# Block forms of the output projection made on GpSimd in an earlier stage, and the norm's sums on ScalarE

## The chip, the cores and the metric

The kernel runs on one core of one Trainium2 chip, as one launch. The time is device microseconds of that core, and the median over several runs. The five engines are named as the profile names them: PE is TensorE (matmuls), DVE is VectorE, ACT is ScalarE, POOL is GpSimd, SP is SyncE, which here only issues DMAs. PEclk is the clock that PE was granted, as a share of full speed.

## The reference

A decoder trunk of two layers over 1024 tokens of 1024 channels. Each layer projects x, runs a main mixer on 1024 channels (layer 0: causal pooling, layer 1: forgetting attention with 16 heads) and a cross-attention of 4 heads of 128 into 256 memory tokens, gates both, and multiplies the 1536 joined channels by `w_out`; then comes a layer norm. What the change touches is the end of layer 1 and its memory attention:

```python
    y_main = main_fn(u_main)
    y_mem = memory_attention(q_mem, mem, w_mem_kv)
    y = jnp.concatenate([y_main * jax.nn.silu(g_main), y_mem * jax.nn.silu(g_mem)], axis=-1)
    return y @ w_out
...
        x = layer_norm(ALPHA * x + y, ln_g[layer], ln_b[layer])

def layer_norm(x, g, b):
    mu = jnp.mean(xf, axis=-1, keepdims=True)
    var = jnp.mean(jnp.square(xf - mu), axis=-1, keepdims=True)
    y = (xf - mu) * lax.rsqrt(var + LN_EPS) * g.astype(jnp.float32) + b.astype(jnp.float32)
```

All arithmetic is float32 outside; inside, a float32 operand is split into a high and a low part of fewer bits, and a product takes three matmuls (high by high, high by low, low by high).

## The kernel before, in words

Layer 1 runs in this order: the memory part (`mem_attention`: keys, values and queries of the memory heads, then a loop over eight row tiles t with `probs(t)`, and two steps behind it `values`), the shared keys and values, the forgetting attention over 16 heads in 8 pairs (`fox`), and the output projection (`Seven.rest`). PE follows an order that is written out by hand (`manual_schedule`), and matmuls of a later stage are filled in between (`Fill`). For the other engines a scheduler sets the order, except for the instructions handed to `keep_in_program_order` (`pin`). Each engine works through its own queue in order, DMA issues included; a wait at the front of a queue holds all that is behind.

In the memory part the softmax runs for each t as: DVE's row maxima (L536, L537), ACT's exponentials (L540), DVE's sums and reciprocals (L543, L544), ACT's and DVE's high and low halves of the probabilities (L546, L547, tile P). Meanwhile weights for the next stage are loaded on SP and split by ACT and DVE (L171 and L172, L198 to L200, tiles w and MK). The outputs of the memory heads (tile V) are gated and stored in DRAM as `y1d[2]` by four DMAs on POOL's queue (L585), then read back at the end.

The output projection multiplies y (1024 by 1536) by W_out (1536 by 1024), both cut in half twice. The 512 memory channels (c = 2) are multiplied in the plain way, in four pairs of row tiles sp = 0 to 3: `heads_of(sp)` issues 48 matmuls for each (L806). The 1024 main channels (c = 0, 1) go in seven products instead of eight: W_out's 8 tiles of 128 rows are 4 sets (k) of 2 x 2 blocks, and of each set seven forms are wanted: the blocks 11, 21, 22 and 12 as "t3" = b22 - b12, and sums of these, "t2", "t4", "t1". Each form of each k is a pair of float16 halves (128 x 2 x 512, 256 KB), scaled by `swo`, a power of two that is known when layer 0's output projection has passed over W_out (L347); 28 pairs in all. In `four` and `block` raw blocks are loaded on SP into rows of the large tile `lines` (A in the profile, L739), summed on POOL, some on DVE (L769), turned into the high half on ACT (L777) and the low half on DVE (L778), into tiles of B, w, MK, R and V as these come free.

For each pair sp, `rows(sp)` makes the halves of y in the same seven forms: sums of absolute values on ACT (L863), added up on DVE (L864), the largest over the partitions through two small PE instructions (L334, DVE L335, PE L337, DVE L338), a scale from it, four sums on POOL (L874), then ACT (L171) and DVE (L172) halves. `seven(sp)` issues seven products of 48 matmuls (L895) and collects them on DVE (L905, L915, L922, L923). `opened` adds the residual to the heads' part (L944). Then `normed` takes mean and variance of each of the two row tiles with two statistics instructions (L1026) and small ones (L1028 to L1036) on DVE, and applies them on ACT and POOL (L1043 to L1045), the last tile on DVE (L1049, L1051). `between(sp, k)` sets which step of `rows` and `normed` lies between which products.

## Time and profile before

| what | us |
|---|---|
| median of 3 runs | 1208.27 |
| lowest and highest of them | 1206.38, 1209.21 |
| the profiled execution's own time | 1205.48 |
| its span, first to last instruction | 1203.8 |
| PE busy in the span | 1163.3 |
| DVE busy | 847.0 |
| ACT busy | 720.2 |
| POOL busy | 360.1 |

The stages that matter here: the memory part of layer 1 from 468 to 592 us, the heads stage of the output projection from 1050 to 1107 us, the seven products from 1107 to 1191 us, and the last norm to 1204 us. In a row of groups stand the line, the engine, the operation, the tile written and those read, the shape, the count, and then busy time, mean ns of one, and idle time of the engine just before them with what ended it. In a timeline row the first number is the start and the second the length, of all the instructions joined in the row where it ends in x2 or more. In a row of waits stand who waited, for whom, the total, the number of times and the longest.

### The profile page before, as it was taken

To read this page: it belongs to the slowest core of one execution; us is meant where nothing else is said; L and a number is where in the kernel's file an instruction comes from. 1 tells how busy PE (TensorE), PEld (TensorE's weight loads), DVE (VectorE), ACT (ScalarE), POOL (GpSimd) and SP (SyncE) were. 2 spreads that over 40 slices of the span, in tenths; PEclk is the share of its full clock that TensorE was granted. 3 is DMA by queue.
4 is the path that set the end of the run, shared out by engine and by line. 5 is a ranking of instruction groups with operands and counts; after the bars stand their busy time and mean duration, and the time that the engine had idled before them with its cause. 6 is when DMAs were issued, how large, how long until landed. Compare 5 with 4: busy or idle time off the path is not lost. (4 is left out here: it accounts for less than half of the span.)

```text
span 1203.8 us, 20044 instructions
## 1 busy us (share of the span) xinstructions
PE 1163.3 (97%) x6908; PEld 658.8 (55%) x6908; DVE 847.0 (70%) x1954; ACT 720.2 (60%) x1597; POOL 360.1 (30%) x476
## 2 busy tenths in 40 slices
PE   8999999999999999999999999999999999998985
PEld 5566766555555556556664555555555545454432
DVE  6744675555755557457655888778778788889898
ACT  6578875875674234566423767667667677765421
POOL 4322001310000000000012554555445445684554
PEclk8999999999999999999999999999999999998998
DMA  7576756854388555355725989979987999884011
GB/s 259 172 244 189 171 102 206 264 164 148 104 307 254 141 157 134 102 147 117 228 89 120 197 188 194 196 162 222 204 176 156 165 234 214 213 271 159 18 53 71
DMA packets 288663, 208.10 MB, mean 173 GB/s; under 512 B 225201, under 2 KB 238641, under 8 KB 288561
## 3 DMA queue, kind: packets, MB, share of 16 engines
q1 hardware_dynamic: 281584, 183.69, 61.2%
q0 software_dynamic: 6976, 23.14, 6.0%
q8 instruction: 54, 0.88, 0.3%
q14 instruction: 49, 0.39, 0.1%
HBM read 120.07 MB, written 22.61 MB: 119 GB/s over the span
## 5 line engine op out<-in xcount | busy, mean ns | idle before, releaser
L388 PE MATMUL pj<-A,w 128*128 128x512 f16 (+2 forms) x2848 | 653.2, 383 | 1.1 <-ACT w L198 1.1
L388 PEld LDWEIGHTS <-w 128*128 128x128 f16 (+1 forms) x2560 | 245.7, 98 | 277.8 <-issue 9.1
L1415 ACT ACTIVATE T<-MK,s 128x512 f32<-128x512 f32 x192 | 111.2, 579 | 65.4 <-DVE s L1407 48.4
L1444 DVE SCALAR_TENSOR_TENSOR P<-T,s,P 128x512 f16<-128x512 f32 x192 | 112.0, 613 | 39.9 <-ACT P L1443 38.1
L1443 ACT ACTIVATE P<-T,s 128x512 f16<-128x512 f32 x192 | 103.0, 576 | 53.4 <-issue 28.9
L1381 POOL TENSOR_SCALAR_AFFINE_SELECT raw<-R 128x256 f32<-128x256 f32 (+3 forms) x128 | 59.8, 469 | 181.1 <-DVE s L1407 100.1
L585 POOL DMA_DIRECT2D y1d<-V x4 | 2.1, 534 | 341.0 <-DMA B<-in_wk_dram 335.1
L199 DVE TENSOR_TENSOR w<-raw,w 128x512 bf16<-128x512 f32 x74 | 52.3, 707 | 60.7 <-ACT w L198 39.6
L352 PE MATMUL L<-A 128*128 128x512 f16 (+3 forms) x384 | 84.7, 326 | 5.9 <-DVE s L1407 5.8
L388 PEld LDWEIGHTS pj<-A,w 128*128 128x128 f32 x352 | 65.1, 188 | 17.3 <-ACT w L198 1.9
L352 PEld LDWEIGHTS <-A 128*128 128x128 f16 x384 | 37.4, 98 | 49.3 <-issue 8.1
L178 POOL TENSOR_TENSOR w<-B,w 128x512 f16<-128x512 f32 x54 | 62.9, 1166 | 4.0
L644 PEld LDWEIGHTS <-T 128*128 128x128 bf16 x384 | 36.9, 98 | 45.8 <-issue 1.9
L198 ACT CAST w<-raw 128x512 fp32r<-128x512 f32 x76 | 46.7, 615 | 24.9 <-DMA raw<-in_win_dram 10.7
L895 PEld LDWEIGHTS <-A 128*128 128x128 f16 x336 | 33.1, 99 | 44.8 <-issue 7.5
L1469 PEld LDWEIGHTS <-V 128*64 128x64 f16 (+1 forms) x1152 | 50.6, 104 | 12.9 <-issue 6.0
L1469 PE MATMUL O<-T,V 128*64 128x128 f16 (+1 forms) x1152 | 57.5, 220 | 0.0
L1407 DVE CUSTOM_DVE_ANT_0 MK<-L,R,scales 128x512 f32<-128x512 f32 x64 | 45.3, 708 | 9.7 <-PE L L352 9.4
L200 ACT CAST w<-raw 128x512 bf16<-128x512 f32 x78 | 48.2, 617 | 3.3 <-PE pj L388 1.9
L258 POOL DMA_DIRECT2D W<-in_win_dram x48 | 26.5, 553 | 55.9 <-ACT W L267 44.2
L540 ACT ACTIVATE P<-L,s 128x256 f32<-128x256 f32 x64 | 29.5, 472 | 22.9 <-DVE s L537 19.4
L267 ACT ACTIVATE W<-W 128x512 f32<-128x512 f32 (+1 forms) x68 | 42.2, 623 | 0.0
(388 smaller groups left out, 2092.6 us busy)
## 6 DMA issues: line engine op xcount, KB each, us to landing
raw<-in_win_dram SPq DMA_DIRECT2D x66, 256.0 KB, 3.5
W<-in_win_dram POOLq DMA_DIRECT2D x48, 256.0 KB, 4.1
A<-in_wout_dram SPq DMA_DIRECT2D x36, 256.0 KB, 4.2
R<-cumd SPq DMA_DIRECT2D x16, 512.0 KB, 4.7
B<-in_win_dram SPq DMA_DIRECT2D x15, 512.0 KB, 5.1
y0d<-Y SPq DMA_DIRECT2D x12, 512.0 KB, 4.1
raw<-in_wout_dram SPq DMA_DIRECT2D x24, 256.0 KB, 2.8
T<-y0d SPq DMA_DIRECT2D x12, 512.0 KB, 4.9
```

The lines of the kernel that those rows point to most:

```text
L178: pin(nc.gpsimd.tensor_tensor(to.lo, src, to.hi, ALU.subtract))
L198: pin(nc.scalar.copy(to.hi, src))
L199: pin(nc.vector.tensor_tensor(to.lo, src, to.hi.bitcast(F32), ALU.subtract))
L200: pin((top or nc.scalar.copy)(to.top, src))
L352: nc.tensor.matmul(acc, a, b, start=i == 0, stop=i == len(terms) - 1)
L388: nc.tensor.matmul(accs[n], a[:, k, :], b[:, pc * 4 + k, n * NH : (n + 1) * NH], start=seen[n] == 1, stop=seen[n] == 3 * KT,)
L1381: tc.keep_in_program_order(nc.gpsimd.affine_select(C[:, :w], R[:, lo:up], [[-1, w]], ALU.is_ge, -NEG, base=w - P, channel_multiplier=1,))
L1407: nc.vector.tensor_tensor_reduce(p[:, lo:up], lg, rows, unq, top, ALU.add, ALU.min, m[:, n : n + 1])
L1415: nc.scalar.activation(e, p[:, lo:up], AF.Exp, bias=top, scale=-1.0, accum_out=sums[:, n, hd % 2, i : i + 1],)
L1443: nc.scalar.activation(pair[:, lo:up], e, AF.Copy, scale=r)
L1444: nc.vector.scalar_tensor_tensor(pair[:, L + lo : L + up], e, r, pair[:, lo:up], ALU.mult, ALU.subtract)
L1469: nc.tensor.matmul(acc[rows, (i % 4) * P : (i % 4) * P + P], v[:, b, 2 * j : 2 * j + (1 if e else 2), :].rearrange("p e d -> p (e d)"), pt ...
```

## The change

The forms of W_out are made earlier. A generator, `blocks_of_w_out`, is handed to layer 1's `mem_attention` as `aside` and stepped at fixed places: before and after the memory keys, behind two of the heads, and at each step t. It works on POOL's queue alone, pinned: for each k it loads four raw blocks (256 KB each), scales them, makes the sums, makes high and low halves with a copy and a subtraction, and stores the seven pairs in a DRAM tensor `w7d`. That is 16 loads, 16 scalings, 16 sums, 28 copies, 28 subtractions and 28 stores.

At the end, `blocks(upto)` loads the 28 pairs on SP, ready for use, into rows of `lines`, and tiles w, V and R. The lines L739 to L778 of raw loads, sums and halves are gone.

Besides, the inputs of the third and fourth heads part are loaded and split before they are asked for, the rows x of the residual too, the gate product of the last head pair's first columns goes straight to where `rows(0)` reads it, and the order of the seven products becomes 11, 12, s2, s1, s3, s4, 22. The small constants of the shared keys' stage move to a row of `lines` and are made ahead of the generator. The loads of R in the attention are pinned from the third head on.

Last, for the first three pairs `normed_pair` replaces `normed`: the sum and the sum of squares of each row tile come from ACT passes with an accumulator, the small instructions work on both tiles at once (two columns), and the result is applied on ACT and POOL for the first tile and on DVE, with two passes of 1024 columns, for the second. The last pair keeps `normed`.

The diff, cut to its core:

```diff
+            every = lines[0][:, 15, :].bitcast(F32)
+            tc.keep_in_program_order(nc.gpsimd.memset(every[:, P : 2 * P], 1.0))
+            tc.keep_in_program_order(nc.gpsimd.affine_select(
+                every[:, :P], every[:, P : 2 * P], [[1, P]], ALU.is_ge, 0.0, base=0, channel_multiplier=-1,
+            ))
+            next(aside)
             for h in range(MH):
                 keys(h)
+            next(aside)
...
             vals(h)
+            if l:
+                next(aside)
...
             for t in range(ST + 2):
                 part = fill.left / (ST + 2 - t)
+                if aside:
+                    next(aside, None)
                 if t < ST:
                     probs(t)
                 if before and t == ST - 2:
...
             fill.pump(float("inf"))
+        if aside:
+            run(aside)
         if last:
             last(1)
...
+    BLOCKS = ("11", "21", "t2", "t1", "t3", "22", "t4")
+
+    def blocks_of_w_out():
+
+        gp, pin = nc.gpsimd.tensor_tensor, tc.keep_in_program_order
+
+        def ask(k):
+            at = [lines[0][:, 4 * (k % 2) + j, :].bitcast(F32) for j in range(4)]
+            for j, r in enumerate(at):
+                pin(nc.gpsimd.dma_start(r, wout[1, j % 2, 4 * (j // 2) + k]))
+            return at
+
+        def scale(rs):
+            for r in rs:
+                pin(nc.gpsimd.tensor_scalar(r, r, swo, 1.0, ALU.mult, ALU.mult))
+
+        asked, turn, done = ask(0), 0, []
+
+        def split(b, k, r):
+            nonlocal turn
+            row = lines[0][:, 8 + turn % 7, :].rearrange("p (e n) -> p e n", e=2)
+            turn += 1
+            pin(gp_copy(row[:, 0], r))
+            pin(gp(row[:, 1], r, row[:, 0], ALU.subtract))
+            done.append((w7d[BLOCKS.index(b), k], row))
+
+        def store():
+            while done:
+                pin(nc.gpsimd.dma_start(*done.pop(0)))
+
+        scale(asked)
+        pin(gp(asked[1], asked[3], asked[1], ALU.subtract))
+        yield
+        for k in range(4):
+            b11, b12, b21, b22 = asked
+            if k < 3:
+                asked = ask(k + 1)
+            if k:
+                scale((b11, b12, b21, b22))
+                pin(gp(b12, b22, b12, ALU.subtract))
+                yield
+                store()
+            split("11", k, b11)
+            pin(gp(b11, b12, b11, ALU.add))
+            split("t3", k, b12)
+            split("21", k, b21)
+            pin(gp(b21, b21, b11, ALU.subtract))
+            yield
+            store()
+            split("22", k, b22)
+            pin(gp(b22, b22, b11, ALU.subtract))
+            split("t2", k, b11)
+            split("t4", k, b21)
+            split("t1", k, b22)
+            yield
+            store()
+
...
-        def block(self, b, f, by=None):
-
-            pin = tc.keep_in_program_order
-            if not self.spare:
-                self.spare.extend(self.pieces())
-            to, r = self.spare.pop(0), f[b]
-            pin(nc.scalar.activation(to.hi, r, AF.Copy, scale=swo))
-            pin(nc.vector.scalar_tensor_tensor(to.lo, r, swo, to.hi, ALU.mult, ALU.subtract))
-            self.w7[b].append(to)
-            if b == "11":
-                self.gp(f["t2"], f["t3"], f["11"], ALU.add, by)
-            elif b == "21":
-                self.gp(f["t4"], f["21"], f["t2"], by=by)
-            elif b == "22":
-                self.gp(f["t1"], f["22"], f["t2"], by=by)
-
...
+        def blocks(self, upto):
+
+            while self.got < upto:
+                for pair in self.pieces():
+                    b, k = BLOCKS[self.got // 4], self.got % 4
+                    tc.keep_in_program_order(nc.sync.dma_start(pair, w7d[BLOCKS.index(b), k]))
+                    self.w7[b].append(Half(pair[:, 0], pair[:, 1]))
+                    self.got += 1
...
+            of = self.load(2, 2, self.more("R", F32))
+            yield
...
+            self.third = Split(MK([P, 4, 2 * P]), MK([P, 2, 4, 2 * P], BF16))
+            self.fourth = self.load(2, 3, sb([P, 4, 2 * P], "P", 4))
+            self.blocks(14)
+            yield
+            hi_lo(self.third, of, True)
+            self.z = [rows_of(x1, sp, self.make[sp]) for sp in range(2)]
...
-            add(z12, self.product(y["s4"], w["22"]), z12)
-            between(2)
             add(u, self.product(y["s2"], w["t2"]), u)
             nc.vector.tensor_tensor(z12, z12, u, ALU.add)
-            between(3)
+            between(2)
             p = self.product(y["s1"], w["t1"])
             add(z12, p, z12)
             add(z22, p, z22)
-            between(4)
+            between(3)
             add(v, self.product(y["s3"], w["t3"]), u)
             nc.vector.tensor_tensor(z22, z22, v, ALU.add)
             nc.vector.tensor_tensor(z21, z21, v, ALU.add)
+            between(4)
+            add(z12, self.product(y["s4"], w["22"]), z12)
...
+                if sp < n - 1:
+                    return normed_pair(sp, zs[sp], gb, dst, self.room[:, 14, :].bitcast(BF16))
                 for a in range(2):
-                    normed(2 * sp + a, zs[sp][a], gb, None, dst, 2 * sp + a < ST - 1)
...
-                self.split(22)
-                w = self.split_last()
+                accs, units = heads_of(2, self.third, (("L", 3), ("pj", 2), ("pj", 2), ("L", 3)))
+                self.blocks(28)
                 next(rows[0])
-                next(w)
                 run(islice(units, 28))
                 next(rows[0])
-                next(w)
                 run(islice(units, 10))
                 next(rows[0])
-                next(w)
                 run(units)
+                self.z.append(rows_of(resid, 3, self.make[3]))
                 zs[2] = opened(2, accs)
                 accs, units = heads_of(3, None, (("T", 2), ("T", 2), ("L", 3), ("O", 1)))
...
+    def normed_pair(sp, z, gb, dst, unread):
+
+            add, ss, v, sd, r, t = (tiny(2) for _ in range(6))
+            for a in range(2):
+                nc.scalar.activation(unread, z[a], AF.Copy, accum_out=add[:, a : a + 1])
+            nc.vector.tensor_scalar(add, add, -1.0 / D, None, ALU.mult)
+            for a in range(2):
+                nc.scalar.activation(unread, z[a], AF.Square, bias=add[:, a : a + 1], accum_out=ss[:, a : a + 1])
+            nc.vector.tensor_scalar(v, ss, 1.0 / D, LN_EPS, ALU.mult, ALU.add)
+            nc.scalar.activation(sd, v, AF.Sqrt)
+            nc.vector.reciprocal(r, sd)
+            nc.vector.tensor_tensor(t, r, r, ALU.mult)
+            nc.vector.tensor_tensor(t, t, v, ALU.mult)
+            nc.vector.tensor_scalar(t, t, -0.5, 1.5, ALU.mult, ALU.add)
+            nc.vector.tensor_tensor(r, r, t, ALU.mult)
+            nc.vector.tensor_tensor(t, add, r, ALU.mult)
+            nc.scalar.activation(z[0], z[0], AF.Identity, bias=t[:, 0:1], scale=r[:, 0:1])
+            nc.gpsimd.tensor_tensor(z[0], z[0], gb[0], ALU.mult)
+            nc.gpsimd.tensor_tensor(z[0], z[0], gb[1], ALU.add)
+            nc.vector.scalar_tensor_tensor(z[1], z[1], add[:, 1:2], gb[0], ALU.add, ALU.mult)
+            nc.vector.scalar_tensor_tensor(z[1], z[1], r[:, 1:2], gb[1], ALU.mult, ALU.add)
+            for a in range(2):
+                nc.sync.dma_start(dst[(2 * sp + a) * P : (2 * sp + a + 1) * P, :], z[a])
 
...
+                to = out_proj.first[1][:, 3, :] if (pr, k) == (7, 0) else o[:, cols]
+                tc.keep_in_program_order(nc.gpsimd.tensor_tensor(to, o[:, cols], g[:, cols], ALU.mult))
...
+            pin = tc.keep_in_program_order if hd > 2 else lambda ins: ins
+            pin(nc.sync.dma_start(R, cumd[hd].partition_broadcast(P)))
...
-        later_tags = iter([("B", 10)] * 3 + [("w", 6)] * 6 + [("MK", 4)] * 2 + [("R", 2)] * 2 + [("V", 4)] * 2 + [("B", 10)] * 2)
+        later_tags = iter([("", k) for k in range(8)] + [("w", 6)] * 6 + [("", k) for k in range(8, 16)] + [("V", 4)] * 2 + [("R", 2)])
```

POOL's queue in the memory part, before: the last loads of weights ahead of it (W), the four stores of the memory heads' output, and the first work of the next stage.

```order
L258 DMA W_2765<-in_wv_dram 128x512 x2
L258 DMA W_2786<-in_wv_dram 128x512 x2
L585 DMA y1d<-V_5065 128x1024
L585 DMA y1d<-V_5066 128x1024
L585 DMA y1d<-V_5067 128x1024
L585 DMA y1d<-V_5068 128x1024
L1264 MEMSET G_6222 128x128
L1265 AFFINE_SELECT G_6222<-G_6222 128x128
L176 TENSOR_SCALAR B_6336<-B_6336,scales 128x512
```

The same place after, where A is the tile `lines`: the start of the generator behind those loads,

```order
L741 DMA A_3344<-in_wout_dram 128x512 x4
L746 TENSOR_SCALAR A_3344<-A_3344,scales 128x512 x4
L763 TENSOR_TENSOR A_3344<-A_3344 128x512
L741 DMA A_3344<-in_wout_dram 128x512 x4
L193 TENSOR_SCALAR A_3344<-A_3344 128x512
L755 TENSOR_TENSOR A_3344<-A_3344 128x512
L775 TENSOR_TENSOR A_3344<-A_3344 128x512
L193 TENSOR_SCALAR A_3344<-A_3344 128x512
L755 TENSOR_TENSOR A_3344<-A_3344 128x512
```

and its end, with the stores of V:

```order
L193 TENSOR_SCALAR A_3344<-A_3344 128x512
L755 TENSOR_TENSOR A_3344<-A_3344 128x512
L193 TENSOR_SCALAR A_3344<-A_3344 128x512
L755 TENSOR_TENSOR A_3344<-A_3344 128x512
L760 DMA w7d<-A_3344 128x1024 x4
L598 DMA y1d<-V_5114 128x1024
L598 DMA y1d<-V_5115 128x1024
```

Between the two pieces stand 74 more rows of the same kinds: the stores of V, which stood right behind the weights' loads, are now behind all the generator's work.

DVE's queue in the heads stage, before, from the halves of the blocks (into MK) to the reduction L335 for the first pair's scale (L944 are the adds of `opened`, L199 a split of y's memory channels):

```order
L778 SCALAR_TENSOR_TENSOR MK_12767<-A_3343,scales,MK_12767 128x512 x2
L778 SCALAR_TENSOR_TENSOR MK_12776<-A_3343,scales,MK_12776 128x512 x2
L769 TENSOR_TENSOR A_3343<-A_3343 128x512
L864 TENSOR_REDUCE yscales<-yscales 128x1
L944 SCALAR_TENSOR_TENSOR A_3343<-A_3343,T_12695 128x512
L944 SCALAR_TENSOR_TENSOR A_3343<-A_3343,T_12696 128x512
L944 SCALAR_TENSOR_TENSOR A_3343<-A_3343,L_12697 128x512
L199 TENSOR_TENSOR T_12876<-T_12873,T_12875 128x1024
L944 SCALAR_TENSOR_TENSOR A_3343<-A_3343,O_12698 128x512
L944 SCALAR_TENSOR_TENSOR G_12865<-G_12865,L_12760 128x512
L944 SCALAR_TENSOR_TENSOR G_12865<-G_12865,pj_12761 128x512
L335 TENSOR_REDUCE yscales<-L_12813 1x1
```

After, the same two reductions of the scale (L864 is now L901) and the adds (now L981):

```order
L199 TENSOR_TENSOR T_12971<-P_12728,T_12970 128x1024
L981 SCALAR_TENSOR_TENSOR B_12758<-B_12758,O_12826 128x512
L901 TENSOR_REDUCE yscales<-yscales 128x1
L981 SCALAR_TENSOR_TENSOR G_12811<-G_12811,L_12879 128x512
L981 SCALAR_TENSOR_TENSOR G_12811<-G_12811,pj_12880 128x512
L335 TENSOR_REDUCE yscales<-L_12924 1x1
L981 SCALAR_TENSOR_TENSOR G_12812<-G_12812,pj_12881 128x512
L338 COPY yscales<-L_12924 128x1
L271 TENSOR_SCALAR yscales<-yscales 128x1
L272 TENSOR_SCALAR yscales<-yscales 128x1
```

The halves and sums of blocks are gone from between, and the reductions stand among adds alone.

ACT's queue among the seven products, before, where the first pair's norm takes a root for each tile (L1030), and applies it (L1043); L171 are halves of y, L907 a product's copy out of its bank:

```order
L1030 ACT_TABLE_LOAD
L1030 ACTIVATE s_13151<-s_13150 128x1
L907 ACTIVATE P_13186<-pj_13187,yscales 128x512
L1030 ACTIVATE s_13171<-s_13170 128x1
L171 ACTIVATE A_12641<-T_13018,yscales 128x512
L171 ACTIVATE A_12641<-T_13020,yscales 128x512
L1043 ACTIVATE G_12686<-G_12686,s_13153,s_13152 128x1024
L171 ACTIVATE A_12641<-raw_13141,yscales 128x512
L863 ACTIVATE A_12641,yscales<-T_13202 128x1024
L863 ACTIVATE A_12641,yscales<-T_13204 128x768
L1043 ACTIVATE G_12687<-G_12687,s_13173,s_13172 128x1024
```

After, with the four sums of `normed_pair` (L1061, L1064) and one root for both tiles (L1066):

```order
L171 ACTIVATE A_12713<-T_12809,yscales 128x512
L1061 ACTIVATE A_12713,s_13219<-G_12753 128x1024
L1061 ACTIVATE A_12713,s_13219<-G_12754 128x1024
L1064 ACTIVATE A_12713,s_13220<-G_12753,s_13219 128x1024
L944 ACTIVATE P_13245<-pj_13246,yscales 128x512
L1064 ACTIVATE A_12713,s_13220<-G_12754,s_13219 128x1024
L171 ACTIVATE A_12713<-T_13071,yscales 128x512
L1066 ACT_TABLE_LOAD
L1066 ACTIVATE s_13222<-s_13221 128x2
L171 ACTIVATE A_12713<-T_13073,yscales 128x512
L171 ACTIVATE A_12713<-raw_13212,yscales 128x512
```

Four passes of 1024 columns stand on ACT between halves of y where two roots stood.

More of the change, by code (lines that the diff above doesn't have):

```diff
@@ L795, in heads @@
+        got = 0
         def heads(self, accs, ys, apart=False):
@@ L963, in rest @@
                 next(rows[0])
+                next(rows[1])
+                self.z.append(rows_of(resid, 2, G))
+                self.blocks(22)
                 accs, units = heads_of(1, self.second, (("T", 2), ("T", 2), ("L", 3), ("O", 1)))
```

118 lines of the change are left out of this document (44 added, 74 removed).

## Prediction

> **What bounds the kernel now.** I read the page first, for the engine that is busy all the time, and then the stages that the change touches: how full each engine is in them, what TensorE (PE) waits for, and the prices of the groups.
>
> ```profile
> span 1203.8 us, 20044 instructions
> PE 1163.3 (97%) x6908; PEld 658.8 (55%) x6908; DVE 847.0 (70%) x1954; ACT 720.2 (60%) x1597; POOL 360.1 (30%) x476
> PEclk8999999999999999999999999999999999998998
> ```
>
> PE is busy for 97% of the span, and its order of instructions is the same before and after. So time is won only where PE stands idle or runs at a lower granted clock, which the last row shows in the two slices around 1085 us, and each new wait of PE is lost whole. The stages, as busy time in each stretch (for each engine us and count, then granted clock, DMA share, GB/s):
>
> ```profile
> core 0: us, PE busy (x) PEld busy (x) DVE busy (x) ACT busy (x) POOL busy (x), PEclk, DMA share, GB/s
> 468.00:530.00 62.00, 61.24 (x366) 36.91 (x364) 32.92 (x66) 34.85 (x62) 0.00 (x0) 1.00 0.51 136
> 530.00:592.00 62.00, 62.00 (x420) 36.77 (x418) 42.49 (x111) 41.16 (x117) 0.00 (x0) 1.00 0.66 148
> 592.00:604.00 12.00, 11.76 (x133) 9.46 (x129) 10.12 (x15) 2.79 (x7) 2.96 (x7) 1.00 1.00 343
> 1050.00:1107.00 57.00, 51.62 (x275) 28.75 (x274) 53.08 (x75) 35.47 (x62) 39.17 (x28) 0.94 0.75 235
> 1107.00:1191.00 84.00, 76.11 (x342) 33.65 (x340) 77.93 (x151) 29.73 (x51) 43.14 (x21) 0.98 0.12 44
> ```
>
> 468 to 592 is layer 2's memory part, with PE full, POOL empty and DVE at 32.92 and 42.49 of 62. 1050 to 1107 is the heads stage and 1107 to 1191 the seven products: there DVE is nearly full (53.08 of 57, 77.93 of 84), and PE loses 5.4 and 7.9 us. PE's waits from 1050 us to the end (total, times, longest):
>
> ```profile
> PE L L337 <- DVE yscales L335: 7.1, 3, 2.5
> PE pj L895 <- DVE G L905: 2.5, 2, 2.3
> PE pj L895 <- DVE A L905: 1.3, 1, 1.3
> PE L L334 <- DVE yscales L864: 1.2, 1, 1.2
> PE O L806 <- DVE G L1488: 0.8, 1, 0.8
> ```
>
> Every wait is for DVE. And in the timeline of PE in the heads stage:
>
> ```profile
> 1077.47 0.61 PE L806 MATMUL L<-B,T 128*128 128x512 bf16 x2
> 1087.48 0.58 PE L337 MATMUL L<-yscales,ones 1*128 1x1 f32 x2 [2.22 <-DVE yscales L335]
> 1087.99 1.22 PE L806 MATMUL L<-B,T 128*128 128x512 f32 x2
> ```
>
> After the 2.22 us of idleness a pair of matmuls takes 1.22 us instead of 0.61: the granted clock falls for some 6 us after a long wait. In the first row of the two, 0.94 of 57 us, that is 3.4 us.
>
> **The change, part by part.**
>
> *Heads stage.* What DVE spends here on the blocks' lo halves (L778, first row) and DVE's and POOL's share of the blocks' sums (L769, second row):
>
> ```profile
> 1050.00:1107.00 57.00, 27.24 (x27) 0.94 0.75 235
> 1050.00:1107.00 57.00, 4.40 (x3) 20.12 (x12) 0.94 0.75 235
> ```
>
> 27.24 + 4.40 = 31.6 of DVE's 53.08 us go, with POOL's 20.12 and the 28 ACT passes of L777. What is left is 21.5 us for 57, so the reductions L864 and L335 stand behind the adds alone, and their waits go: of L337's 7.1 us the longest, 2.5, lies in the seven stage, so 4.6 here, and 3.4 of clock that follows them. The O bank's 0.8 waits for an instruction (L1488) that the change leaves alone, and stays. Gain 8.0; if half the clock loss stays, 6.3; 5 if one of the two waits only shrinks by half besides. What is late next is the transpose L334 behind ACT's sums, which had time.
>
> *Seven stage.* All waits of PE here are 2.5 (L337) + 2.5 + 1.3 (L905) + 1.2 (L334) = 7.5, and the clock (0.98 of 84) 1.7: at most 9.2, when DVE never holds PE. What normed costs DVE here, rows of L1026, L1034 and L1036 in this order, and the price of a 1024-wide pass, which is what normed_pair puts on DVE, twice a pair, and of ACT's:
>
> ```profile
> 1107.00:1191.00 84.00, 9.50 (x14) 0.98 0.12 44
> 1107.00:1191.00 84.00, 5.34 (x6) 0.98 0.12 44
> 1107.00:1191.00 84.00, 4.10 (x6) 0.98 0.12 44
> L1049 DVE SCALAR_TENSOR_TENSOR G<-G,s,P 128x1024 f32<-128x1024 f32 x7 | 8.9, 1277 | 0.0
> L1043 ACT ACTIVATE G<-G,s,s 128x1024 f32<-128x1024 f32 x4 | 4.9, 1234 | 6.1 <-DVE s L1036 6.1
> ```
>
> Three pairs' sums are 12 of the 14 L1026: 8.1 us go. The tiny ones (9.4 us for 12, since they wait for POOL) are joined to one per pair: half, 4.7, goes. Six passes of 1.277 come: 7.7. So DVE wins 5.1 here, plus 1.0 of the two last L778, plus what it waited for POOL, which makes 2 passes for each pair instead of 4. DVE at 77.9 - 6.1 = 71.8 of 84 still has bursts, and between ACT's sums (4 x 1.234 = 4.9 a pair, off PE's path) and DVE's applications new idleness appears. Of 9.2 I take the share that the relief of 6.1 gives: 5; ends 1 (bursts hold PE as now) and 9.2. The last pair's norm, after 1191, keeps its form: 0.
>
> *The ends of loads.* 16 raw loads and 28 stored pairs of 256 KB are 4.2 and 7.3 MB: 3.1 MB more at the 343 GB/s of the third row are 9 us of DMA time, against a quarter of 57 us, 14, that is idle. Cost 0; without that cover, a landing would hold a product for some us, which belongs to the range. The earlier loads and splits of y (third and fourth heads input), the other order of products and the gate product without its own small load move DVE work of the same amount forward: 0, with DVE's new room as cover.
>
> *Memory part.* The prices on POOL, from the rows of the same forms:
>
> ```profile
> L176 POOL TENSOR_SCALAR B<-B,scales 128x512 f32<-128x512 f32 x54 | 37.8, 700 | 3.3 <-DMA B<-in_win_dram 3.3
> L193 POOL TENSOR_SCALAR w<-B 128x512 f16<-128x512 f32 x54 | 33.3, 617 | 23.8 <-PE pj L388 19.7
> L178 POOL TENSOR_TENSOR w<-B,w 128x512 f16<-128x512 f32 x54 | 62.9, 1166 | 4.0
> L874 POOL TENSOR_TENSOR raw<-T,T 128x512 f32<-128x512 f32 x3 | 3.8, 1275 | 9.2 <-DVE A L172 5.3 <-DVE yscales L864 3.9
> L258 POOL DMA_DIRECT2D W<-in_win_dram x48 | 26.5, 553 | 55.9 <-ACT W L267 44.2
> ```
>
> 16 scalings x 0.70 + 16 sums x 1.275 + 28 copies x 0.617 + 28 differences x 1.166 = 11.2 + 20.4 + 17.3 + 32.6 = 81.5 us in 88 instructions (0.93 each), and 44 DMA issues x 0.553 = 24.3: 106 us. They can begin when the scale is there, and stand ahead of the y1d stores in POOL's queue:
>
> ```profile
> 467.71 0.15 DVE L347 TENSOR_SCALAR scales<-scales 128x1 f32<-128x1 f32 x1
> 595.03 0.54 POOL L585 DMA_DIRECT2D y1d<-V  x1 [335.05 <-DMA B<-in_wk_dram]
> ```
>
> 468 + 106 = 574, 21 us ahead of the first store: by itself 0. But POOL and DVE get in each other's way, as the timelines of now show where POOL is dense:
>
> ```profile
> 1018.48 0.69 DVE L199 TENSOR_TENSOR V<-B,V 128x512 bf16<-128x512 f32 x1
> 1020.87 3.27 DVE L199 TENSOR_TENSOR MK<-A,MK 128x512 bf16<-128x512 f32 x2
> 1064.34 6.79 POOL L769 TENSOR_TENSOR A<-A 128x512 f32<-128x512 f32 x4
> 1065.56 1.06 DVE L199 TENSOR_TENSOR P<-P,P 128x512 bf16<-128x512 f32 x1
> ```
>
> One such DVE instruction takes 0.69 alone, 1.06 beside POOL's sums and 1.64 (3.27 for two) beside its differences: 0.37 to 0.95 more. POOL's sums take 1.70 instead of 1.275: 0.42 more. DVE has these of two inputs in SBUF, the first two rows from 468 to 530, the others from 530 to 592:
>
> ```profile
> L172 DVE SCALAR_TENSOR_TENSOR w<-raw,scales,w 128x512 f16<-128x512 f32 x11 | 8.2, 748 | 4.9 <-ACT w L171 4.9
> L199 DVE TENSOR_TENSOR w<-raw,w 128x512 bf16<-128x512 f32 x10 | 6.9, 688 | 5.6 <-PE L L388 3.8 <-ACT w L198 1.5
> L547 DVE SCALAR_TENSOR_TENSOR P<-P,s,P 128x256 f16<-128x256 f32 x32 | 13.5, 480 | 2.2 <-ACT P L546 2.2
> L172 DVE SCALAR_TENSOR_TENSOR w<-raw,scales,w 128x512 f16<-128x512 f32 x7 | 5.1, 746 | 0.3 <-ACT w L171 0.2
> L172 DVE SCALAR_TENSOR_TENSOR MK<-raw,scales,MK 128x272 f16<-128x272 f32 x4 | 1.7, 496 | 0.0
> ```
>
> The 21 before 530 find 29 us of idle DVE and cost nothing. The 32 + 7 + 4 = 43 behind: 43 x 0.37 = 16 us and 43 x 0.95 = 41 us, against DVE's idle 62 - 42.5 = 19.5. The low end is covered: 0. The high end leaves 21 us that PE, without idle time of its own, must wait, since the softmax of the next tile reads through DVE. I take 0.6, somewhat under the middle (POOL also issues DMAs, a quarter of its time, when it takes nothing from DVE): 43 x 0.6 = 26, less 19.5: 6.5 us. POOL's own end: at most 64 meetings (with the 21 such instructions before 530) x 0.42 = 27 later, 601, against 595 + 6.5: covered. DMA: 44 x 256 KB = 11.5 MB at 343 GB/s are 34 us of the engines over 106, which lifts 0.51 and 0.66 to 0.83 and 0.98; weights' loads land later, with a prefetch ahead of them: 0, at worst some 3 us.
>
> The rule that bears on this is the Trainium skill's, SBUF — State Buffer, "Who interferes with whom": a DVE instruction with two SBUF inputs contends with a GpSimd instruction that reads SBUF, and the lock is exclusive, so the one that comes second waits out the other's whole instruction. The rows above agree in kind (1.64 against 0.69). Were every one of the 43 to come second to a whole POOL instruction of 0.93 us, the sum would be 40 - 19.5 = 20 us of cost instead of 6.5, which is the rival D below.
>
> **Sum.** Tail 8 + 5 = 13 won, 6.5 lost: 6.5 won. The profiled execution took 1205.5 us (span 1203.8 and 1.7 around it), which lies 2.8 below the median of the runs, 1208.3. 1205.5 - 6.5 = 1199, and as a median 1202.
>
> **Rivals.**
> A, the forecast: 1202, its own range 1197 to 1206.
> B, the memory part is free (the DVE's lengthening stays under 0.45 each, inside its 19.5 us) and the seven stage gains all: 8 + 9.2 = 17, 1191. For it: POOL would be done 21 us early, and DVE stands idle 29 us before 530. Against it: L547s come in fours, back to back, so each meets another POOL instruction.
> C, the seven stage gains 1 only, since ACT's four passes and DVE's two make a chain whose bursts hit the adds L905: 8 + 1 - 6.5 = 2.5, 1206, no change within the bound. For it: PE waits for L905 for 3.8 us now, beside a POOL that keeps half its norm passes.
> D, the other side: the lock makes DVE the bound of 530 to 592. At 0.95 each it costs 21: 13 - 21 = 8 slower, 1216. It turns slower once each of the 43 grows by more than (13 + 19.5) / 43 = 0.76 us; between the ends some 1212. For it: POOL's queue is dense there for the first time, and the one row with two differences side by side shows 0.95.
>
> **How the numbers follow.** A change of up to 0.2% (2.4 us) is about what a measurement of this kernel can't tell from none. A 0.46, B 0.16, C 0.17, D 0.21. Faster: A's greater part, B: 0.60. Within 0.2% (1205.9 to 1210.7): C and the upper edge of A and the lower of D: 0.18. Slower: 0.22. The range leaves out the best of B and the worst of D: 1191 to 1214.
>
> **What would show it.** In the changed kernel's profile: no wait of PE on L335 in the heads stage and a clock of 1.00 there (8 us); DVE under 90% in the seven stage, and its waits at the adds halved (5); POOL busy some 85 to 110 us in 468 to 600, L547 at 0.9 to 1.2 us instead of 0.48, and 6 us of new PE waits on DVE or on ACT's exponentials between 530 and 604. The prediction is wrong if L547 stays near 0.48 (B), if L547 goes over 1.25 or the y1d stores leave later than 602 because POOL is late (D), or if PE's waits on L905's adds stay at 3.8 us (C).

## The result, and the profile after

| | median us | lowest to highest | runs |
|---|---|---|---|
| before | 1207.39 | 1204.72 to 1209.21 | 6 |
| after | 1213.53 | 1211.23 to 1215.98 | 6 |

The ratio is 1.0054, 95% interval 1.0034 to 1.0073: the change makes the kernel about 6.5 us slower, where 6.5 us faster was forecast. The profiled execution after took 1212.01 us (span 1210.3).

PE executes as many matmuls as before, and up to the seven products in the same order. So the start of the matmul with the same number in the two traces tells how far the kernel has fallen behind at that place:

| place (matmul in PE's order) | before us | after us | behind |
|---|---|---|---|
| 2300th, end of layer 0 | 461.1 | 459.0 | -2.1 |
| 2770th, in the memory part's loop | 541.5 | 541.0 | -0.5 |
| 2977th, end of the loop | 569.7 | 585.1 | +15.3 |
| 3240th, next stage begun | 602.2 | 618.2 | +16.0 |
| 6300th, end of the attention | 1051.5 | 1068.0 | +16.5 |
| 6571st, end of the heads stage | 1107.9 | 1116.4 | +8.5 |
| last one | 1190.5 | 1194.6 | +4.1 |
| end of the span | 1203.8 | 1210.3 | +6.5 |

So the memory part costs 18 us, the heads stage wins 8.0, the seven stage 4.4, and the end, after the last matmul, loses 2.4 (16.0 and 0.5 in the attention make up the 16.5 behind). The 2.1 us at the start lie in layer 0, which the change leaves alone. Without them the parts come to 8.6 us, so it is chance that the two profiled executions differ by the same 6.5 us as the runs.

The same stretches as busy times, after (columns as in the prediction; the last three rows are the heads stage, the seven products and the end, where they lie now):

```profile
468.00:530.00 62.00, 59.97 (x353) 35.50 (x352) 37.86 (x64) 34.90 (x61) 60.07 (x68) 1.00 0.71 216
530.00:592.00 62.00, 52.39 (x322) 29.66 (x320) 52.87 (x87) 31.47 (x91) 53.06 (x62) 0.92 0.73 176
1066.60:1115.00 48.40, 47.60 (x273) 27.29 (x271) 23.08 (x48) 18.49 (x34) 15.51 (x16) 1.00 0.94 325
1115.00:1194.80 79.80, 76.02 (x344) 33.83 (x342) 66.55 (x118) 39.38 (x68) 26.54 (x15) 0.98 0.16 59
1194.80:1210.30 15.50, 0.15 (x1) 0.00 (x0) 12.01 (x25) 1.19 (x3) 4.12 (x3) 0.58 0.27 102
```

From 530 to 592 PE was busy for all of 62.00 us and is now for 52.39, at a clock of 0.92 instead of 1.00: 9.6 us idle and 5.0 us of slower clock. DVE went from 42.49 to 52.87 and POOL from 0 to 53.06. Further on the heads stage runs at a clock of 1.00 with DVE at 23 of 48 us. The longest waits of PE in the whole span, after:

```profile
PE L L543 <- ACT P L549: 8.6, 4, 2.6
PE L L352 <- DVE s L1466: 6.0, 8, 1.6
PE L L337 <- DVE yscales L335: 3.2, 2, 2.4
```

The second was there before (5.8). The first is new: the next tile's logits (L543) wait for a bank that the exponentials (L549, before L540) still read. What keeps these, from the timeline of one step of the loop, in order of time:

```profile
537.41 1.16 POOL L755 TENSOR_TENSOR A<-A 128x512 f16<-128x512 f32 x1
537.61 4.69 DVE L556 SCALAR_TENSOR_TENSOR P<-P,s,P 128x256 f16<-128x256 f32 x4
538.64 1.33 POOL L775 TENSOR_TENSOR A<-A 128x512 f32<-128x512 f32 x1
539.95 0.79 POOL L193 TENSOR_SCALAR A<-A 128x512 f16<-128x512 f32 x1
540.82 1.20 POOL L755 TENSOR_TENSOR A<-A 128x512 f16<-128x512 f32 x1
542.22 0.58 DVE L546 TENSOR_SCALAR s<-s 128x2 f32<-128x2 f32 x1
542.84 0.47 ACT L549 ACTIVATE P<-L,s 128x256 f32<-128x256 f32 x1 [3.49 <-DVE s L546]
543.91 0.96 PE L543 MATMUL L<-MK,B 128*128 128x256 f32 x6 [1.86 <-ACT P L549]
544.71 6.38 PE L388 MATMUL pj<-A,w 128*128 128x512 f16 x21
```

The four L556 take 4.69 us where the four L547 of before took 1.7 (4 x 0.42). The small L546 stands behind them. ACT waits 3.49 us for it and PE 1.86 us for ACT, and then PE's next 21 matmuls take 6.38 us, where 21 x 0.216 = 4.5 are usual: eight of them ran at half clock (0.427 us apart instead of 0.216). By groups over the loop, after:

```profile
L556 DVE SCALAR_TENSOR_TENSOR P<-P,s,P 128x256 f16<-128x256 f32 x32 | 26.1, 872 | 2.3 <-ACT P L555 2.2
L546 DVE TENSOR_SCALAR s<-s 128x2 f32<-128x2 f32 x16 | 7.4, 465 | 0.0
L172 DVE SCALAR_TENSOR_TENSOR w<-raw,scales,w 128x512 f16<-128x512 f32 x7 | 6.7, 973 | 0.3 <-ACT w L171 0.2
```

0.872 instead of 0.480 us, 0.973 instead of 0.746, and 0.465 for L546, which before was L537:

```profile
L537 DVE TENSOR_SCALAR s<-s 128x2 f32<-128x2 f32 x16 | 2.5, 161 | 0.0
```

The end, with the two adds that follow the last products beside POOL's two passes of the third pair's norm:

```profile
1190.64 2.37 POOL L1074 TENSOR_TENSOR G<-G,P 128x1024 f32<-128x1024 f32 x1 [15.51 <-ACT G L1073]
1192.49 1.06 DVE L957 TENSOR_TENSOR B<-B,P 128x512 f32<-128x512 f32 x1
1193.08 2.67 POOL L1075 TENSOR_TENSOR G<-G,P 128x1024 f32<-128x1024 f32 x1
1193.47 2.83 DVE L958 TENSOR_TENSOR B<-B,P 128x512 f32<-128x512 f32 x1
```

### The profile page after: what moved, and what is told of

Same layout as the page of the kernel before. It is cut to its first block, busy times and chain, and to the rows that moved or that the text cites. A ratio compares the mean times of both kernels' runs of the same rounds, so it can differ in the third digit from the quotient of the medians.

```text
span 1210.3 us, 20105 instructions
## 1 busy us (share of the span) xinstructions
PE 1165.4 (96%) x6908; PEld 658.8 (54%) x6908; DVE 832.7 (69%) x1899; ACT 714.8 (59%) x1587; POOL 436.6 (36%) x589
## 5 line engine op out<-in xcount | busy, mean ns | idle before, releaser
L388 PE MATMUL pj<-A,w 128*128 128x512 f16 (+2 forms) x2848 | 656.5, 384 | 1.4 <-DVE G L405 0.5
L388 PEld LDWEIGHTS <-w 128*128 128x128 f16 (+1 forms) x2560 | 246.6, 98 | 280.6 <-issue 13.6
L199 DVE TENSOR_TENSOR w<-raw,w 128x512 bf16<-128x512 f32 x74 | 54.8, 740 | 61.0 <-ACT w L198 42.6
L388 PEld LDWEIGHTS pj<-A,w 128*128 128x128 f32 x352 | 64.9, 188 | 17.5 <-ACT w L198 1.9
L549 ACT ACTIVATE P<-L,s 128x256 f32<-128x256 f32 x64 | 29.6, 473 | 39.2 <-DVE s L546 37.1
L746 POOL TENSOR_SCALAR A<-A,scales 128x512 f32<-128x512 f32 x16 | 16.3, 1032 | 93.4 <-DVE scales L347 93.3
L439 PE MATMUL pj<-T,w 128*128 128x256 bf16 (+1 forms) x344 | 41.2, 279 | 2.0 <-DVE w L199 1.0
```

The lines of the kernel that those rows point to most:

```text
L199: pin(nc.vector.tensor_tensor(to.lo, src, to.hi.bitcast(F32), ALU.subtract))
L388: nc.tensor.matmul(accs[n], a[:, k, :], b[:, pc * 4 + k, n * NH : (n + 1) * NH], start=seen[n] == 1, stop=seen[n] == 3 * KT,)
```

## The experiments

All times are medians, each with its ratio to the kernel before, timed on the same chip. All but one, which says so, start from the changed kernel. Losses and gains of a part are by the start of the same matmuls, as in the table above. Some traces hold only 6868 of the 6908 matmuls; there the matching ones are taken.

### Arithmetic or DMA

Arithmetic left out:

```diff
-            pin(gp_copy(row[:, 0], r))
-            pin(gp(row[:, 1], r, row[:, 0], ALU.subtract))
+        gp = lambda *a: None        # sums too; scalings for the first k alone
```

> The generator's loads and stores stay, its arithmetic (scalings but the first four, sums, copies, subtractions) is left out, so the output projection multiplies by other data. Theory 1 (DVE is held by POOL's instructions in the memory part): the 18 us that PE loses up to the end of the memory part come back, the stretch from 468 us to the first values matmul of the next stage falls from 144.7 to about 128.5 us, L556 is at 0.48 us, and the time is about 1213.5 - 17 = 1196 us. Theory 2 (the 11.5 MB of extra DMA traffic and the DMA issues on POOL's queue delay weights or the y1d stores): the time stays near 1213.

Measured: 1206.40 us, 0.9988 (0.9976 to 1.0001). Neither number came. PE's longest wait in its trace:

```profile
PE L L388 <- DMA A<-A: 8.6, 2, 7.0
```

Without arithmetic between them the loads and stores went out close together, and a transposing DMA of the activations came late: 11 us lost, all before the 2770th matmul. From there to the end of the loop, where the changed kernel loses 15.8 us, this one loses nothing, and L543 doesn't wait. So the arithmetic is what costs in the loop; the 11 us are this kernel's own.

DMAs left out:

```diff
+                if k < 2:
                     pin(nc.gpsimd.dma_start(r, wout[1, j % 2, 4 * (j // 2) + k]))
...
+                if not stored:
                     pin(nc.gpsimd.dma_start(to, of))
```

> All arithmetic on POOL stays, but of its DMAs only the loads of the first two k and one store remain (the output projection reads one stored pair 28 times). Theory 1: the memory part stays as long as in the changed kernel or a little longer where POOL works without pauses, 142 to 148 us from 468; POOL ends some 20 us earlier, so if density alone decides, the late steps t are free: time 1207 to 1213 us. Theory 2: the memory part falls back to some 129 us, the time to about 1197.

Measured: 1210.97 us, 1.0025 (1.0008 to 1.0042). The memory part still loses 13.9 us (18.0 in the changed kernel), nearly all by the 2850th matmul; POOL was done earlier, and the last steps of the loop are free. Theory 2 falls.

### What lets DVE in

Every instruction of the generator cut in two:

```diff
+        def cut(f, *args):
+            for c in range(2):
+                cols = slice(c * (NH // 2), (c + 1) * (NH // 2))
+                pin(f(*(x[:, cols] for x in args)))
...
-            pin(gp_copy(row[:, 0], r))
+            cut(gp_copy, row[:, 0], r)
```

> Same results: each POOL instruction of the generator is split into two of 256 columns. Theory 1, with DVE waiting out the rest of a whole POOL instruction: a DVE instruction of L556 waits about half as long (0.85 falls to 0.65 us mean), PE gets back 6 to 12 of the 18 us, unless POOL, some 15 us longer in all, holds back the y1d stores: time 1202 to 1208 us. Rival 3 (DVE and POOL share a bandwidth, so that only the bytes count): no gain, 1213 us or more.

Measured: 1242.66 us, 1.0299 (1.0271 to 1.0326): 29 us slower than the change, against both. In its timeline DVE first, POOL behind:

```profile
481.02 8.46 DVE L199 TENSOR_TENSOR w<-raw,w 128x512 bf16<-128x512 f32 x1 [0.79 <-ACT w L198]
```
```profile
480.16 0.79 POOL L193 TENSOR_SCALAR A<-A 128x256 f16<-128x256 f32 x2
480.91 1.29 POOL L745 TENSOR_TENSOR A<-A 128x256 f16<-128x256 f32 x2
482.17 1.39 POOL L748 TENSOR_TENSOR A<-A 128x256 f32<-128x256 f32 x2
...
486.28 2.65 POOL L745 TENSOR_TENSOR A<-A 128x256 f16<-128x256 f32 x4
488.88 1.67 POOL L772 DMA_DIRECT2D w7d<-A  x3
```

An instruction of 0.69 us takes 8.46, through fourteen of POOL's, and ends when POOL stops for its stores. With both halves' copies ahead of both subtractions no POOL instruction needs the one right before it, and they follow without a gap. That made theory 1b: DVE gets in only where POOL runs dry. The next kernel has the same instructions in another order:

```diff
-            cut(gp_copy, row[:, 0], r)
-            sub(row[:, 1], r, row[:, 0])
+            for c in range(2):
+                cols = slice(c * (NH // 2), (c + 1) * (NH // 2))
+                pin(gp_copy(row[:, 0, cols], r[:, cols]))
+                pin(nc.gpsimd.tensor_tensor(row[:, 1, cols], r[:, cols], row[:, 0, cols], ALU.subtract))
```

> Same results, and the same 256-wide POOL instructions as in the half-width kernel (1242.7 us), except that a half's subtraction stands right behind its copy, on which it depends, instead of both copies ahead of both subtractions. Theory 1b (DVE gets in only where POOL runs dry, because the next POOL instruction needs the result of the last one or issues a DMA; POOL instructions that don't depend on each other follow without a gap and keep DVE out): L172's mean falls from 1.87 us to 1.0 or less, the time to 1208 to 1222 us. Rival (each POOL instruction costs DVE something, so that their number decides): as before, 1235 to 1245 us.

Measured: 1214.00 us, 1.0062 (1.0039 to 1.0085), 29 us less for the order alone. Up to the end of the loop it loses 6 us instead of 17; then POOL, which is done only at 607 us, holds back the y1d stores, and PE waits 5.8 us in one piece behind what needs the stored tiles V again. Stores as gaps:

```diff
-            done.append((w7d[BLOCKS.index(b), k], row))
+            pin(nc.gpsimd.dma_start(w7d[BLOCKS.index(b), k], row))
```

> Same results: each pair is stored right behind its subtraction, so 28 DMA issues of 0.55 us stand between POOL's arithmetic instead of 3 or 4 together. Theory 1b: DVE finds a gap after every two or three POOL instructions, L556 falls from 0.87 to some 0.6 us, and PE gets back 4 to 12 us: 1202 to 1210 us. Rival (the sum of POOL's arithmetic beside DVE decides, wherever the gaps lie): 1212 to 1215 us.

Measured: 1218.12 us, 1.0093 (1.0076 to 1.0111), slower than the change: a miss. One place of its timeline, DVE and then POOL:

```profile
574.52 2.08 DVE L546 TENSOR_SCALAR s<-s 128x2 f32<-128x2 f32 x1
```
```profile
574.09 0.59 POOL L756 DMA_DIRECT2D w7d<-A  x1 [0.41 <-POOL A L755]
574.70 1.28 POOL L775 TENSOR_TENSOR A<-A 128x512 f32<-128x512 f32 x1
575.95 0.63 POOL L193 TENSOR_SCALAR A<-A 128x512 f16<-128x512 f32 x1
576.66 1.16 POOL L755 TENSOR_TENSOR A<-A 128x512 f16<-128x512 f32 x1
```

DVE came while POOL issued a DMA, and still waited out that issue, the sum behind it and the copy; it ended at 576.60, in the gap ahead of a subtraction that needs the copy. The DVE instruction ahead of it ended only at 574.60, 0.10 us before the sum began; but another L546, at 556.29, took 1.84 us with 0.4 us of the issue still to go. So at these places a single issue was no gap. It is no rule: the 8.46 us above ended among POOL's stores, and in the kernel before this one four L556 ran at 0.42 us each, as without POOL's work, while POOL issued loads:

```profile
541.34 1.67 DVE L556 SCALAR_TENSOR_TENSOR P<-P,s,P 128x256 f16<-128x256 f32 x4
```
```profile
540.57 1.64 POOL L753 DMA_DIRECT2D A<-in_wout_dram  x3
```

Why the stores between the arithmetic cost more is not shown.

### The norm and the end

```diff
+            for a in range(2) if sp == 2 else (1,):
+                nc.vector.scalar_tensor_tensor(z[a], z[a], add[:, a : a + 1], gb[0], ALU.add, ALU.mult)
+                nc.vector.scalar_tensor_tensor(z[a], z[a], r[:, a : a + 1], gb[1], ALU.mult, ALU.add)
+            if sp < 2:      # ACT and POOL as before
```

> Same results: for the third pair the norm of both tiles is applied on DVE, so POOL has no passes beside the last adds. If the end (15.5 us after the last product instead of 13.1) is late because the adds L957 and L958 wait out POOL's 1024-wide passes (2.83 us instead of 0.69, twice), the end falls to about 13 us and the time by 1.5 to 2.5 us less what two more passes of 1.28 us cost the last products (0 to 2.5): 1211 to 1213 us. If the end is late for another reason, 1213 to 1216 us.

Measured: 1213.20 us, 1.0046 (1.0031 to 1.0061). In the trace the end loses 0.3 us instead of 2.4, and the seven stage wins 3.5 instead of 4.4: the cause of the late end is POOL's passes, and the net, 1.2, is too small for the runs to tell. Old norm:

```diff
-                if sp < n - 1:
-                    return normed_pair(sp, zs[sp], gb, dst, self.room[:, 14, :].bitcast(BF16))
```

> Same results: the changed kernel with the old norm (statistics on DVE, POOL passes for both tiles) for the first three pairs. If normed_pair is what won the 4 us of the seven stage, it goes back to 83 or 84 us, and the end, late by POOL's passes of the third pair, stays near 15 us or goes back to 13: 1213 to 1218 us. If the seven stage won by the blocks' absence and the other order alone, it stays at 80 us: 1211 to 1214 us. The memory part stays as it is in both.

Measured: 1215.49 us, 1.0079 (1.0058 to 1.0099). The seven stage wins nothing (0.3 us lost instead of 4.4 won) and the end loses 0.2: normed_pair is all of the seven stage's gain, and all of the end's loss. The other way round, the kernel before with normed_pair and the end on DVE, and nothing else:

> Same results: the kernel before, with normed_pair for the first three pairs and the third pair's norm applied on DVE; nothing else of the change. From the old norm put back into the changed kernel (seven stage 4.7 us longer, end 2.3 us shorter) and from the end with the third pair on DVE (2.2 us shorter there, 0.9 longer in the seven stage): 3 to 4 us faster than before, 1203.5 to 1205 us. If normed_pair needs DVE's relief by the blocks' absence to win, 1206 to 1209 us.

Measured: 1206.40 us, 0.9988 (0.9971 to 1.0005), not told from before. In its profiled execution the seven stage wins 0.6 us only. DVE is relieved there too (68.42 us busy of 82.00), and PE's waits in that stage fall from 7.7 to 5.0 us, but the granted clock is 0.95 instead of 0.98, which takes back about as much (an estimate: 0.03 x 82 = 2.5 us). The heads stage ahead of it is 3.7 us longer than before, with longer waits at L337 (6.0 us instead of 4.5), which were not followed up. So normed_pair alone did not win here; whether the blocks' absence or another part of the change is what it needs was not separated.

### Putting gaps in, and getting the stores out

```diff
+            scale(b11)
+            split("11", k, b11)      # copy, subtraction, store
+            scale(b12)
+            ask(k + 1, 0)            # one load
+            scale(b22)
...
```

> Same results: stores and loads spread singly between the generator's instructions, the scalings apart from each other, each as near as can be ahead of an instruction that needs it; and the third pair's norm applied on DVE. Theory 1b: the memory part's loss falls from 18 to 5 to 10 us, the end by 1 to 2: 1199 to 1207 us. Rival (sum of POOL's arithmetic): 1211 to 1213 us.

Measured: 1215.20 us, 1.0067 (1.0053 to 1.0080): a miss: the loop (2770th to 2977th matmul) loses 16.1 us, no less than the changed kernel's 15.8, and why is not shown. This kernel and those below also apply the third pair's norm on DVE. Next the chains, 256 wide, with the 44 DMAs merged into 16:

```diff
+            for c in halves:
+                scale(b22, c)
+                scale(b12, c)
+                pin(gp(b12[:, c], b22[:, c], b12[:, c], ALU.subtract))
+                form(1, b12, c)      # copy and subtraction of this half
...
+            store(k, 0, 3)           # three pairs in one DMA
```

> Same results: in the generator POOL's 256-wide instructions are put in chains, each form's scaling, sum, copy and subtraction of one half behind each other, and the loads and stores are merged into 16 DMA issues instead of 44; the third pair's norm is applied on DVE. Theory 1b (DVE gets in where a POOL instruction waits for the result of the one ahead, not at a DMA issue): the memory part loses 3 to 9 us instead of 18, POOL is done before 600 us, and the time is 1200 to 1206 us. Rival (DMA issues or their count are what matters): close to the fully wide chain of the same run. Rival (each POOL instruction costs): 1215 us and more.

Measured: 1216.02 us, 1.0071 (1.0048 to 1.0094), far from the forecast, and yet the loop is healed. Its groups and PE's waits:

```profile
L556 DVE SCALAR_TENSOR_TENSOR P<-P,s,P 128x256 f16<-128x256 f32 x32 | 19.9, 679 | 2.2 <-ACT P L555 2.2
```
```profile
PE pj L1294 <- DVE G L1303: 10.3, 1, 10.3
PE L L543 <- ACT P L549: 1.9, 3, 1.2
```

From the 2300th matmul to the end of the loop it loses 2.8 us instead of 17.4. Then it loses 17: 5.7 by the 3100th matmul, beside POOL's work that goes on, and most of the rest because POOL is done at 616 us and the stores of V, which are behind it in the queue, start at 616.4 us, 14 after the first V is ready. With 512 columns:

> Same results: as the chained kernel, but with 512-wide instructions. Theory 1b: gaps are as far apart as a pair of whole instructions, so DVE waits about as long as in the changed kernel where it meets POOL (L556 0.75 to 0.9 us), but POOL is done some 15 us earlier for want of DMA issues, so the last steps t are free: 1206 to 1211 us. If the width doesn't matter: within 2 us of the 256-wide chain.

Measured: 1212.22 us, 1.0038 (1.0022 to 1.0053): L556 at 0.936 us, the loop loses 13.1 us (2.3 in the 256-wide kernel over the same matmuls), and POOL waits for V before it stores it. Width matters, where the order gives gaps. Scalings on ACT, to end POOL's work sooner:

```diff
-            pin(nc.gpsimd.tensor_scalar(r[:, c], r[:, c], swo, 1.0, ALU.mult, ALU.mult))
+                pin(nc.scalar.activation(two, two, AF.Copy, scale=swo))
```

> Same results: as the chained kernel with 256-wide instructions, but the 16 scalings are 8 passes of 1024 columns on ACT, and nothing in the generator waits for a step of the loop. POOL's work falls from 121 to some 95 us and ends near 570 us, so the y1d stores leave on time. If the meeting with the loop is what costs: 2 to 5 us of loss in the memory part, 1199 to 1204 us. If POOL's work costs wherever it lies, or ACT's passes hold back the queries' copies: 8 us and more, 1206 to 1211 us.

> Same results: as the early kernel, with 512-wide instructions, so POOL's work is some 80 us and ends near 555 us. If the meeting with the loop is what costs: two or three steps t are hit, at 1.5 to 2 us each: 3 to 6 us of loss, 1200 to 1205 us. If gaps in POOL's stream matter more than its length: 3 us or more behind the 256-wide one of the same run.

Measured: 1217.08 (1.0075, 1.0061 to 1.0089) and 1224.51 us (1.0129, 1.0103 to 1.0155). In the first, two rows of waits:

```profile
ACT A L750 <- DMA A<-in_wout_dram: 11.1, 2, 5.8
PE L L543 <- ACT P L549: 15.5, 3, 12.3
```

The scalings (L750), pinned in ACT's queue, waited there for loads that POOL issues, with the exponentials behind them. Both kernels say nothing on the question put to them. The stores moved alone, on SP's queue and on ACT's:

```diff
-                tc.keep_in_program_order(nc.gpsimd.dma_start(yd[:, h, :], ys[h]))
+                tc.keep_in_program_order(nc.sync.dma_start(yd[:, h, :], ys[h]))
```

> Same results: the chained kernel (256-wide, merged DMAs, third pair's norm on DVE), with the four y1d stores on SP's queue. If the two parts named are all of the memory part's loss: the stores leave at 600 to 611 us, ACT's wait for them falls from 15 us to 3 or 4, the memory part loses 3 to 5 us in all, and the time is 1198 to 1202 us, faster than before. If POOL's work that goes on until 616 us costs there too, or SP's later loads are held by the stores: 1203 to 1208 us.

> Same results: as the chained kernel, with the four y1d stores on ACT's queue, where ACT waits for V in any case before its next copies. The same 1198 to 1202 us if ACT has nothing else to do there; 1203 to 1208 us if the waits for V hold the halves of MK (L171) and with them the first matmuls of the next stage.

Measured: 1203.80 us, 0.9972 (0.9962 to 0.9983), and 1203.55, 0.9980 (0.9963 to 0.9997). By the ratios they are 3.4 and 2.4 us faster than before, the second only just outside the noise, and 9 to 10 us faster than the change. The memory part on SP's queue:

```profile
530.00:592.00 62.00, 56.84 (x370) 32.80 (x368) 48.93 (x102) 39.67 (x115) 51.49 (x83) 1.00 0.78 195
592.00:625.00 33.00, 29.58 (x279) 22.95 (x278) 20.20 (x38) 6.83 (x20) 22.08 (x31) 1.00 0.77 262
```
```profile
ACT V L1301 <- DMA y1d<-V: 7.8, 2, 6.2
```

The clock is 1.00 again with POOL as busy in the loop as after (51.49 against 53.06). The loss is 2.8 us in the loop and 6.4 behind it, 9.2 in all by the end of the attention, against the 3 to 5 forecast for this kernel. The stores leave from 598 us on, but land 7 to 11 us later (5.3 to 6.9 in the chained kernel). That is not what costs most: on ACT's queue they land after 5.9 to 8.8 us, and the loss behind the loop is 6.7. And 4.2 of the 6.4 us are there by the 3100th matmul, ahead of the stage whose copies (L1301) wait for the stores. There PE waits for DVE (3.3 us at L388), which still meets POOL, as in the four halves for MK, first before and then on SP's queue:

```profile
586.00 1.73 DVE L172 SCALAR_TENSOR_TENSOR MK<-raw,scales,MK 128x272 f16<-128x272 f32 x4
```
```profile
591.35 3.25 DVE L172 SCALAR_TENSOR_TENSOR MK<-raw,scales,MK 128x272 f16<-128x272 f32 x4
```

So by these rows most of what is left is POOL's late work, and the changed kernel, whose POOL is done at 585 us, loses only 0.6 us from the 2977th to the 3240th matmul. For the last 2 us it was not separated from the stores.

## Why the prediction was wrong

**The heads stage was right.** 8.0 forecast, 8.0 measured, by the steps named: the clock is 1.00 there, and L337's waits in this stage are down from 4.5 us to what this row shows.

```profile
PE L L337 <- DVE yscales L335: 0.8, 1, 0.8
```

That the sum came out to the tenth is luck: 0.8 us of L337 stayed that was to go, and the O bank's 0.8 went that was to stay.

**The seven stage was right in size**, 5 forecast and 4.4 measured, and in kind: PE's waits for DVE there fell from 7.7 to 3.7 us. But DVE was relieved by 11.4 us (77.93 to 66.55), not 6.1, so the size is in part luck. All of the gain hangs on normed_pair, and by the kernel before with normed_pair that alone is not enough.

**The end was mis-sized.** "The last pair's norm keeps its form: 0" overlooked the pair ahead of it. The third pair's two POOL passes moved behind ACT's four sums and met the last adds: 2.4 us, shown by the kernel that takes them away (0.3).

**The memory part was the step that failed.** It cost 18.0 us, not 6.5, and yet the price of a meeting, 0.6 us, was too high: L556 grew by 0.39 over the loop, L172 into w by 0.23, and L172 into MK not at all. That makes 32 x 0.39 + 7 x 0.23 = 14 us for the 43, less than DVE's 19.5 us of idle time, and by the prediction's own line the part would have been free. So what failed is the subtraction in "43 x 0.6 = 26, less 19.5". It took DVE's idle time as a pool that pays for the first 19.5 us. But PE waits for a chain (L546, L549, L552, L556), and much of DVE's idle time lies where DVE waits for that chain itself, so it can't make up for the chain's growth: DVE is busy for 52.87 of 62 us and PE still loses 14.6. The chain has some slack of its own: with L556 at 0.679 us the loop loses only 2.8. Two more things were left out. The clock falls to half behind three of the four waits at L543, as it was read off the heads stage and not carried over: 5.0 us of the 18. And L546, with one input in SBUF, was not among the 43, though it stands at the head of the chain and went from 0.161 to 0.465 us. A slip without effect: the row that the prediction calls 0.69 alone lies beside a scaling on POOL, L176; the price holds all the same, by L199's 0.688 from 468 to 530 us.

**The rivals.** D named the place and the mechanism. That its bound of 21 us lies near the 18 measured is in part luck: its condition, over 0.76 us more for each of the 43, was not met and not needed. B's condition, under 0.45 us each, was met, and the memory part was not free; both conditions rest on the same subtraction. The memory part alone turned the sign: 18 lost is more than the 13 forecast for the tail, and than the 10 that it won. The y1d stores left at 610.6 us, later than the 602 named as a sign of D, but not because POOL was late: it was done and waited 25.6 us for V. They became the bound in the chained kernels.

**The rule.** The Trainium skill, SBUF — State Buffer, "Who interferes with whom", has the one that comes second wait out the other's whole instruction. By the 8.46 us through fourteen POOL instructions that is a lower bound here: what was waited out is a run of instructions without a gap. The same section lists tensor_scalar among those that can take the shared ports with one input; L546's 0.465 us against 0.161 agrees with it, and the prediction had not used it.

## What to carry to other kernels

Work put on an idle engine is not free if it can hold up a busy one: price it on the chain that the bounding engine waits for, don't pay for it out of the busy engine's idle time, and add the clock that a wait costs. If such work has to lie there, what helped here was to let each instruction need the one before it, to keep the instructions short, and to put nothing behind them in the same queue that others wait for. With the DMAs merged and the third pair's norm on DVE, that turned 6.5 us slower into about 3 us faster, without moving the work.

## What was not expected of the hardware

The order of the same instructions on POOL alone changed the time by 29 us (1242.66 against 1214.00). A DVE instruction of 0.69 us was kept for 8.46 us, until POOL stopped for its stores. Elsewhere DVE came in where POOL waited for its own last result. A DMA issue let it in at some places (four L556 at 0.42 us each) and not at others (2.08 us for an instruction of 0.16), and what decides is open. That the gap is what lets it in is read from these traces; the lock itself no row shows.
